# One fused decoder block on one core: a second home for transposed weights, later transposes, and the memory operands prepared elsewhere

## The chip, the cores and the metric

The kernel runs on one core of a Trainium2 chip. A core has TensorE (PE: matmuls, with a separate track PEld for loading the stationary operand), VectorE (DVE), ScalarE (ACT), GpSimd (POOL) and SyncE (SP, which here only issues DMAs). The metric is the device time of one execution in microseconds, as the median of several runs.

## The reference, cut to what matters

One layer over 512 positions of width 1024: self-attention with 16 heads of 64 (8 dilated, 8 block-sparse), a projection `w_out`, a cross-attention of 4 heads over 256 memory positions, and a gated MLP with a causal convolution, each with RMSNorm ahead and a residual add behind.

```python
u  = rmsnorm(h, g_mix);  qa, ka, va, qb, kb, vb = split(u @ w_in)
y  = concat([rmsnorm(dilated(qa, ka, va)), rmsnorm(moba(qb, kb, vb))])
h  = h + y @ w_out
m  = rmsnorm(mem, g_mem)                       # 256 x 1024
km, vm = split(m @ w_kv)                       # memory keys, memory values
h  = h + softmax((rmsnorm(h) @ w_q) km.T / 16) vm @ w_o
h  = h + (silu(conv3(rmsnorm(h) @ w_gate)) * (rmsnorm(h) @ w_up)) @ w_down
```

## The kernel before, in words

Everything is kept feature-major: a tile holds 128 features by 512 positions. Each fp32 operand is held as a rounded part (`hi`, fp32r, written by ACT) and a remainder (`lo`, written by DVE or POOL), and each product is three matmuls: hi by hi, hi by lo, lo by hi (`fgroup`, L263 to L268). Weights arrive in chunks of 128 x 1024 through three `stage` buffers; `Weights.tick` splits the next chunk beside the matmuls of the present one (ACT at L88, DVE or POOL at L97), and a finished split issues the DMA three chunks on. All of these DMAs, the bias strips (`load_strip`) and the copies of K go through SP's queue, in the order of the program.

The order on every engine is written out by hand (`manual_schedule`). What follows a matmul group, such as an evacuation, is put into a list, `Later`, and emitted a few steps further on; each group of matmuls is one `L.step()`.

**Self-attention** runs in 18 slots, one per head and two to finish. In slot s the head s has its scores made (S, three pieces: `s_steps`, L658, four score tiles), head s-1 its probabilities transposed (T, three groups of 4, 3 and 3 transposes: `t_steps`, L704), and head s-2 its output (O, four pieces: `o_steps`, L729). Between these stand steps of filler, as many as `PACE` prescribes: the projections `q1`, `k1` ... `k7`, two groups of V, then the memory keys `km0` to `km7` and the memory values `vm0` to `vm3`. The string `ORDER` says where in the slot each piece stands. Softmax of a score piece: DVE reduces (L683), ACT exponentiates (L688), DVE takes reciprocals (L693), and DVE (tiles 2 and 3) or POOL (tiles 0 and 1, the last piece) multiplies by them (L695). The first transposes need tiles 0 and 1. A transposed group is evacuated from PSUM into `pts`: ACT writes `pt0h`, `pt1h`, `pt2h` (L249), DVE `pt0l` and so on (L254). There is one set of `pts`; the O pieces of the head read it.

**Memory operands.** In the unit `k7` the two halves of the transposed memory come in as two chunks of the weight stream (`raw`), and `mem_prep(k)` scales and splits tile k into `X[k][:, 0, :]`, where the normalised stream has been until then, right after `k7` has read it (ACT L251, DVE L261). `km` units multiply these (moving width 256); `vm_unit(c)` takes two chunks of weights, makes 256 columns for two position tiles with 24 matmuls each, and evacuates each on its own. All fillers put their sums into two PSUM banks, tag `acc`; S, T, O and norms share a ring of six.

**After it** comes `w_out` (L819): per output tile a sum `pa` over the first four tiles of Y and `pb` over the last four. They are scaled by the two norms RA and RB, and added to the residual `h`: POOL L832 and DVE L840. RB is made inside this phase (`norm_stages`: two matmuls against ones, L301 and L302; the second waits for a DVE subtraction, L254). `h` is loaded once at the start and stays in memory for the whole kernel.

Of the kernel before, what the change touches and what calls it, by code (L numbers as in the profile page):

```python
# [31 lines left out]
ORDER = "OSOTOSTOST"  # L32
# [17 lines left out]
def bf(ap):  # L50
    return ap.bitcast(F32)
# [121 lines left out]
def block_kernel(tc, xT, x_tok, memT, mem_tok, w_in, w_out, w_q, w_km, w_vm, w_o, w_gu, w_dn, vecs, relT, onehot,  # L173
                 addend, out):
    nc = tc.nc
    with ExitStack() as ctx:
        perm = ctx.enter_context(tc.tile_pool(name="perm", bufs=1))
        wp = ctx.enter_context(tc.tile_pool(name="wp", bufs=1))
# [24 lines left out]
        chunks += [(memT[0], "raw"), (memT[1], "raw")]  # L203
# [17 lines left out]
        nc.sync.dma_start(h[0], xT[0])  # L221
        W.dma(0)
        nc.sync.dma_start(h[1], xT[1])
        W.dma(1)
        for k in (2, 3):
            nc.sync.dma_start(h[k], xT[k])
# [140 lines left out]
        def x_split(k):  # L367
            copy(Xh[k], h[k], col(C_MIX + k))
            scaled_lo(Xl[k], h[k], col(C_MIX + k), Xh[k])
# [40 lines left out]
        for k in range(KT):  # L410
            if k % 2 == 0:
                w = W.take()
            for j in XL.get(k, ()):
                nc.sync.dma_start(h[j], xT[j])
# [29 lines left out]

        Q, K, VM = {}, {}, {}
# [12 lines left out]
        def qk_unit(p, is_k):  # L458
            hook = p == 7 and is_k
            w = W.take()  # L460
            ps = bank("acc")
            for k in range(KT):
                if hook and k == 0:
                    mem_start()
                proj(w, k, ps, Xh[k], Xl[k])
                if hook:
                    L.chain(*mem_prep(k), d=1)
                yield
# [76 lines left out]
        def mem_start():  # L545
            W.lo_eng = tuple(engs[c] for c in LOM)
            VM["st"] = [W.raw(), W.raw()]

        def mem_prep(k):

            src = VM["st"][k // 4][:, (k % 4) * M:(k % 4) * M + M]
            hi, lo = X[k][:, 0, 0:M], X[k][:, 0, M:2 * M]
            return (lambda: copy(hi, src, col(C_MEM + k)),
                    lambda: scaled_lo(lo, src, col(C_MEM + k), hi))

        def km_unit(m):
            w = W.take()
# [16 lines left out]
        def vm_unit(c):  # L574
# [5 lines left out]
            w = [W.take(), W.take()]  # L580
            for t in range(2):
                ps = bank("acc")[:, :256]
                for k in range(KT):
                    wh, wl = w[k // 4]
                    ws = slice((k % 4) * 256, (k % 4) * 256 + 256)
# [685 lines left out]
```

## Time and profile before

| what | value |
|---|---|
| median of 3 runs | 796.68 us (796.01 to 797.83) |
| the profiled execution | 796.25 us |
| its span, first to last instruction | 794.5 us |
| PE busy, share of the span | 97% |
| DVE, ACT, POOL busy | 62%, 49%, 20% |
| mean granted TensorE clock | 0.997 |

The span is followed by lines for groups of instructions, waits and DMAs. A matmul's duration in the trace includes the time that it spends in the pipe behind others, so successive matmuls overlap, and their pace is read from start to start. A bracket behind a row is the time for which the engine stood idle before it and the instruction that ended the wait.

### The profile page before, as it was taken

Reading aid. Unit: us, or ns where it says so; the run is one execution under the profiler, and the core shown is the slowest. Engines: PE = TensorE matmul, PEld = TensorE weight load, DVE = VectorE, ACT = ScalarE, POOL = GpSimd, SP = SyncE. Lnnn points to the kernel's source line nnn. Section 1 sums busy time; section 2 is a strip of 40 time slices with the busy share of each in tenths; the row PEclk is TensorE's granted clock in tenths of the full one; section 3 lists DMA queues with packets and bytes.
Section 4 is the critical chain, followed back from the end, with each engine's and each line's share of the span. In section 5 each row is a group of like instructions: output and inputs, shape, how many; then the busy total and the mean of one; then the engine's idle time right before and its main releaser. Section 6 shows DMA issues by size and latency. Waiting matters only on the chain.

```text
span 794.5 us, 10594 instructions
## 1 busy us (share of the span) xinstructions
PE 772.7 (97%) x3916; PEld 653.9 (82%) x3916; DVE 491.7 (62%) x895; ACT 388.7 (49%) x763; POOL 162.6 (20%) x161
## 2 busy tenths in 40 slices
PE   9999999999999999999999999999999999999995
PEld 7878989877898887888888888888888888888884
DVE  4657676678886987756476765665665664333324
ACT  5856666776767543544355533334333343322322
POOL 1057465663646243000030000000000000000001
PEclk9999999999999999999999999999999999999998
DMA  9545243343534322211232323223223233333303
GB/s 344 198 133 138 78 145 93 109 112 123 161 134 131 108 80 85 75 53 54 80 106 92 104 97 106 99 87 104 91 98 106 88 92 100 99 93 100 99 21 106
DMA packets 27108, 85.86 MB, mean 108 GB/s; under 512 B 3072, under 2 KB 5248, under 8 KB 26672
## 3 DMA queue, kind: packets, MB, share of 16 engines
q1 hardware_dynamic: 25696, 83.90, 32.8%
q10 hardware_dynamic: 1232, 1.12, 0.4%
q8 instruction: 31, 0.51, 0.3%
q14 instruction: 21, 0.17, 0.1%
q0 software_dynamic: 128, 0.17, 0.1%
HBM read 78.84 MB, written 2.14 MB: 102 GB/s over the span
## 4 chain that ended last, share of the span: by engine, by line
PE 77%; DVE 11%; ACT 6%; issue 2%; POOL 2%; DMA 1%; DVEq 0%; POOLq 0%; ACTq 0%
PE acc L267 15%; PE acc L266 15%; PE acc L268 15%; PE s L267 6%; PE s L266 6%; PE s L268 6%; DVE lo L97 2%; ACT P L688 2%; PE o L739 1%; DVE tmp L257 1%; PE t L710 1%; DVE P L695 1%; DVE P L683 1%; ACT hi L88 1%; PE acc L531 1%
## 5 line engine op out<-in xcount | busy, mean ns | idle before, releaser
L88 ACT ACTIVATE hi<-stage 128x512 fp32r<-128x512 f32 (+1 forms) x264 | 151.9, 616 | 173.0 <-PE acc L267 126.6
L97 DVE TENSOR_TENSOR lo<-stage,hi 128x512 fp32r<-128x512 f32 (+1 forms) x211 | 154.8, 764 | 59.4 <-ACT hi L88 59.2
L266 PE MATMUL acc<-X,hi 128*128 128x512 f32 (+1 forms) x416 | 159.5, 384 | 1.1 <-DVE tmp L257 1.1
L268 PE MATMUL acc<-X,lo 128*128 128x512 f32 (+1 forms) x416 | 155.5, 374 | 0.0
L267 PE MATMUL acc<-X,hi 128*128 128x512 f32 (+1 forms) x368 | 137.3, 373 | 1.8 <-DVE X L261 1.5
L268 PEld LDWEIGHTS acc<-X,lo 128*128 128x128 f32 x416 | 78.2, 188 | 14.2
L266 PEld LDWEIGHTS acc<-X,hi 128*128 128x128 f32 x416 | 78.4, 188 | 13.8 <-ACT P L688 1.0
L267 PEld LDWEIGHTS acc<-X,hi 128*128 128x128 f32 x368 | 69.3, 188 | 13.1 <-DVE X L261 3.1
L97 POOL TENSOR_TENSOR lo<-stage,hi 128x512 fp32r<-128x512 f32 x53 | 71.6, 1368 | 27.3 <-ACT hi L88 25.7
L266 PE MATMUL s<-X,hi 128*128 128x512 f32 x192 | 75.1, 391 | 0.0
L268 PE MATMUL s<-X,lo 128*128 128x512 f32 x192 | 74.7, 389 | 0.0
L266 PE MATMUL acc<-G,hi 128*128 128x512 f32 (+1 forms) x198 | 72.9, 368 | 0.0
L268 PE MATMUL acc<-G,lo 128*128 128x512 f32 (+1 forms) x198 | 72.3, 365 | 0.0
L267 PE MATMUL acc<-G,hi 128*128 128x512 f32 (+1 forms) x198 | 72.3, 365 | 0.0
L267 PE MATMUL s<-X,hi 128*128 128x512 f32 x176 | 68.5, 389 | 0.0
L688 ACT ACTIVATE P<-P,st 128x512 f32<-128x512 f32 (+1 forms) x64 | 35.6, 557 | 39.9 <-DVE st L683 39.7
L1072 DVE SCALAR_TENSOR_TENSOR c<-a,vec,c 128x512 f32<-128x512 f32 x44 | 33.1, 752 | 25.2 <-ACT c L1067 24.4
L1062 POOL MEMSET a<- 128x2 f32 x22 | 2.1, 99 | 214.8 <-DVE c L1072 214.0
L266 PEld LDWEIGHTS acc<-G,hi 128*128 128x128 f32 x198 | 37.3, 188 | 6.2
L266 PEld LDWEIGHTS s<-X,hi 128*128 128x128 f32 x192 | 36.0, 187 | 7.7 <-issue 0.2
L268 PEld LDWEIGHTS acc<-G,lo 128*128 128x128 f32 x198 | 37.3, 188 | 6.1
L267 PEld LDWEIGHTS acc<-G,hi 128*128 128x128 f32 x198 | 37.3, 188 | 6.0
(249 smaller groups left out, 1498.8 us busy)
## 6 DMA issues: line engine op xcount, KB each, us to landing
stage<-in_w_gu_dram SPq DMA_DIRECT2D x44, 512.0 KB, 3.3
stage<-in_w_in_dram SPq DMA_DIRECT2D x23, 512.0 KB, 3.5
stage<-in_w_dn_dram SPq DMA_DIRECT2D x16, 512.0 KB, 3.5
strip<-scr SPq DMA_DIRECT2D x16, 256.0 KB, 3.6
stage<-in_w_km_dram SPq DMA_DIRECT2D x8, 512.0 KB, 3.3
stage<-in_w_vm_dram SPq DMA_DIRECT2D x8, 512.0 KB, 3.4
stage<-in_w_out_dram SPq DMA_DIRECT2D x8, 512.0 KB, 3.2
stage<-in_w_q_dram SPq DMA_DIRECT2D x8, 512.0 KB, 3.2
```

The costliest lines, as they stand in the source:

```text
L88: self.nc.scalar.activation(self.hi[i][:, a:b], self.stage[i][:, a:b], AF.Copy)
L97: self.lo_eng[part].tensor_sub(self.lo[i][:, a:b], self.stage[i][:, a:b], bf(self.hi[i][:, a:b]))
L257: nc.vector.tensor_mul(dst, a, b)
L266: nc.tensor.matmul(ps, wh[:, w0:w0 + P], xh, start=first, stop=False)
L267: nc.tensor.matmul(ps, wh[:, w0:w0 + P], xl, start=False, stop=False)
L268: nc.tensor.matmul(ps, wl[:, w0:w0 + P], xh, start=False, stop=last)
L531: nc.tensor.matmul(ps, Xh[k][:, ts], wh[:, ws], start=(k == 0), stop=False)
L683: nc.vector.tensor_tensor_reduce(v, src, sb[:, :n][:, ::-1], -0.125, 3e38, OP.add, OP.min, accum_out=st[:, i:i + 1])
L688: nc.scalar.activation(v, v, AF.Exp, scale=-1.0, bias=st[:, i:i + 1], accum_out=st[:, 4 + i:5 + i])
L695: engs[NME[i]].tensor_scalar(v, v, st[:, 8 + i:9 + i], None, op0=OP.mult)
L710: nc.tensor.transpose(ps[:, c * P:(c + 1) * P], pt[:, PO[i] + kb * P:PO[i] + (kb + 1) * P], ident)
L1072: nc.vector.scalar_tensor_tensor(v["c"], v["a"][:, 6 + o:6 + o + S], col(C_CW + o * FT + f), v["c"], op0=OP.mult, op1=OP.add)
```

## The change

`ORDER` puts the four O pieces of a slot ahead of the three T pieces. `pts` exists twice, and heads take turns. The memory no longer comes through the weight stream: four quarters of it are loaded into a small tile `mr` and split into a tile `XM` of its own, emitted 68, 90, 112 and 134 steps on in `Later`, between slots 3 and 7. `XM` takes the room of the input `x`, whose last reader is the split at the start; when the memory values are done, the room goes to `h`, which is loaded again from `xT`: eight DMAs on SP's queue, ahead of the loads that follow there. `vm_unit` has a moving width of 512: one chunk holds two tiles k of 512 columns, and the two position tiles have their sums open over four chunks, in the two `acc` banks for the first half and in two banks of the ring for the second. The norm RA has its stages 5 steps apart in place of 3. The scratch set aside for POOL's DMA descriptors is 2048 bytes.

```diff
-ORDER = "OSOTOSTOST"
+ORDER = "OOSOOTSTST"
...
-        chunks += [(memT[0], "raw"), (memT[1], "raw")]
...
-        hh_ = perm.tile([P, KT, S], F32, name="h")
-        h = [hh_[:, k, :] for k in range(KT)]
+        x_ = hp.tile([P, KT, S], F32, tag="H", name="x")
+        x = [x_[:, k, :] for k in range(KT)]
...
+        XM = hp.tile([P, KT, 2 * M], F32R, tag="H", name="xm")
+        def mem_prep(j):
+            v = {}
+            def p0():
+                v["t"] = tp.tile([P, 2 * M], F32, tag="mr", bufs=1, name=f"mr{j}")
+                nc.sync.dma_start(v["t"], memT[j // 2][:, (j % 2) * 2 * M:(j % 2 + 1) * 2 * M])
+            def p1(i):
+                hi, src = XM[:, 2 * j + i, 0:M], v["t"][:, i * M:(i + 1) * M]
+                copy(hi, src, col(C_MEM + 2 * j + i))
...
+            L.chain(p0, d=68 + 22 * j)
+            L.chain(lambda: p1(0), lambda: p2(0), lambda: p1(1), lambda: p2(1), d=80 + 22 * j, gap=2)
...
-                fgroup(ps, w, k, X[k][:, 0, 0:M], X[k][:, 0, M:2 * M], k == 0, k == KT - 1)
+                fgroup(ps, w, k, XM[:, k, 0:M], XM[:, k, M:2 * M], k == 0, k == KT - 1)
...
+            ps = {}
+            for j in range(4):
+                w = W.take()
+                for t in range(2):
+                    if j == 0:
+                        ps[t] = bank("acc" if c == 0 else "s")
+                    for i in range(2):
+                        k = 2 * j + i
+                        xh = XM[:, k, t * P:(t + 1) * P]
+                        xl = XM[:, k, M + t * P:M + (t + 1) * P]
+                        ws = slice(i * 512, i * 512 + 512)
+                        nc.tensor.matmul(ps[t], xh, w[0][:, ws], start=(k == 0), stop=False)
+                        nc.tensor.matmul(ps[t], xl, w[0][:, ws], start=False, stop=False)
+                        nc.tensor.matmul(ps[t], xh, w[1][:, ws], start=False, stop=(k == KT - 1))
...
+        pts = [[tuple(ap_.tile([P, n], F32R, name=f"pt{g}{z}{e}") for z in "hl")
+                for g, n in enumerate((512, 384, 512))] for e in range(2)]
...
-                ra_tok = L.chain(*norm_stages(SSQ[0], SSQ[0], S, 512), gap=3)
+                ra_tok = L.chain(*norm_stages(SSQ[0], SSQ[0], S, 512), gap=5)
...
+        hh_ = hp.tile([P, KT, S], F32, tag="H", name="h")
+        h = [hh_[:, k, :] for k in range(KT)]
+        for k in range(KT):
+            nc.sync.dma_start(h[k], xT[k])
...
-    nc = _bacc.Bacc("TRN2", target_bir_lowering=False, num_devices=1)
+    nc = _bacc.Bacc("TRN2", target_bir_lowering=False, num_devices=1, dynamic_dma_scratch_size=2048)
```

How this moves instructions is shown at three places. The first is PE in slot 2, up to the first transposes of head 1 (`t<-ident,P1`; `o<-pt..` are O pieces of head 0, `acc` rows are filler). Before:

```order
L739 MATMUL o_37_667<-pt1h_428,V0_137 128x384
L739 MATMUL o_37_667<-pt1l_429,V0_137 128x384
L266 MATMUL acc_35_644<-X5_111,hi9_553 128x512
L267 MATMUL acc_35_644<-X5_111,hi9_553 128x512
L268 MATMUL acc_35_644<-X5_111,lo9_587 128x512
L266 MATMUL acc_35_644<-X6_112,hi9_553 128x512
L267 MATMUL acc_35_644<-X6_112,hi9_553 128x512
L268 MATMUL acc_35_644<-X6_112,lo9_587 128x512
L710 MATMUL t_39_700<-ident_85,P1_573 128x128 x4
```

After the change, the same transposes:

```order
L750 MATMUL o_37_679<-pt2h0_434,V0_140 128x256
L750 MATMUL o_37_679<-pt2l0_435,V0_140 128x256
L552 MATMUL acc_40_731<-hi10_656,X0_109 128x256
L553 MATMUL acc_40_731<-hi10_656,X0_109 128x256
L554 MATMUL acc_40_731<-lo10_682,X0_109 128x256
L552 MATMUL acc_40_731<-hi10_656,X1_110 128x256
L553 MATMUL acc_40_731<-hi10_656,X1_110 128x256
L554 MATMUL acc_40_731<-lo10_682,X1_110 128x256
L721 MATMUL t_42_741<-ident_88,P1_590 128x128 x4
```

They stood behind the second O piece (`pt1`) and now stand behind the last (`pt2`).

The second place is DVE in slot 8, where head 7 is transposed and head 8 scored (`pt0l` and `pt1l` are the transposed remainders, `P` the score tiles). Before:

```order
L695 TENSOR_SCALAR P_1523<-P_1523,st_1524 128x512
L254 TENSOR_TENSOR pt0l<-t_1546,pt0h 128x512
L257 TENSOR_TENSOR tmp_1565<-acc_1485,rx_138 128x512
L683 ISA P_1523,st_1524<-s_1567,strip_1226 128x384
L683 ISA st_1524 128x1
L514 TENSOR_TENSOR Q_1557<-tmp_1565,Q_1557 64x512
L693 RECIPROCAL st_1524<-st_1524 128x1
L695 TENSOR_SCALAR P_1523<-P_1523,st_1524 128x384
L254 TENSOR_TENSOR pt1l<-t_1580,pt1h 128x384
```

After:

```order
L706 TENSOR_SCALAR P_1567<-P_1567,st_1568 128x512
L771 TENSOR_TENSOR y_1589<-o_1548,tmp_1590 64x512
L258 TENSOR_TENSOR tmp_1600<-acc_1522,rx_141 128x512
L535 TENSOR_TENSOR Q_1592<-tmp_1600,Q_1592 64x512
L694 ISA P_1567,st_1568<-s_1616,strip_1266 128x384
L694 ISA st_1568 128x1
L255 TENSOR_TENSOR pt0l_437<-t_1602,pt0h_436 128x512
L704 RECIPROCAL st_1568<-st_1568 128x1
L706 TENSOR_SCALAR P_1567<-P_1567,st_1568 128x384
```

The remainder `pt1l` stood behind the reciprocal and the multiplication of a score piece; now a remainder stands ahead of these two.

The third place is DVE at the end of self-attention (`vml` are memory values; the `ssy` rows and the two ahead of the first of them make the norm RA; the last row is the subtraction for RB's second matmul; the row before it is the first `pa` times RA). Before:

```order
L312 TENSOR_SCALAR tmp_2861<-tmp_2861 128x512
L257 TENSOR_TENSOR ssy_944<-tmp_2861,tmp_2860 128x512
L760 TENSOR_TENSOR y_2750<-o_2792,tmp_2884 64x512
L97 TENSOR_TENSOR lo_2899<-stage_2757,hi_2892 128x512
L261 SCALAR_TENSOR_TENSOR Y_124<-y_2750,vec,Y_124 128x512
L261 SCALAR_TENSOR_TENSOR vml<-acc_2864,small,vmh 128x256
L97 TENSOR_TENSOR lo_2935<-stage_2814,hi_2921 128x512 x2
L257 TENSOR_TENSOR tmp_2948<-acc_2919,ssy_944 128x512
L254 TENSOR_TENSOR tmp_2957<-ssy_1946,tmp_2946 128x512
```

After:

```order
L97 TENSOR_TENSOR lo_2803<-stage_2718,hi_2792 128x512
L262 SCALAR_TENSOR_TENSOR vml<-s_2690,small,vmh 128x512
L262 SCALAR_TENSOR_TENSOR vml<-s_2708,small,vmh 128x512
L312 SCALAR_TENSOR_TENSOR tmp_2814<-t_2783,tmp_2814 128x512
L313 TENSOR_SCALAR tmp_2814<-tmp_2814 128x512
L258 TENSOR_TENSOR ssy_909<-tmp_2814,tmp_2813 128x512
L97 TENSOR_TENSOR lo_2852<-stage_2752,hi_2840 128x512 x2
L258 TENSOR_TENSOR tmp_2865<-acc_2838,ssy_909 128x512
L255 TENSOR_TENSOR tmp_2874<-ssy_1946,tmp_2863 128x512
```

The three rows of RA and two wide evacuations now stand close ahead of RB's subtraction; before, RA was done ahead of the last evacuation of Y.

## Rows read from the trace of the kernel before

**Rows 1.** The page, section 1: busy time, share of the span, instructions.
```profile
PE 772.7 (97%) x3916; PEld 653.9 (82%) x3916; DVE 491.7 (62%) x895; ACT 388.7 (49%) x763; POOL 162.6 (20%) x161
```
**Rows 2.** Windows: length, busy (x count) PE, PEld, DVE, ACT, POOL, clock, DMA share, GB/s.
```profile
150.00:200.00 50.00, 46.87 (x256) 38.90 (x256) 37.94 (x91) 34.80 (x82) 25.79 (x23) 1.00 0.38 116
...
450.00:500.00 50.00, 50.00 (x222) 41.42 (x221) 30.88 (x47) 20.66 (x34) 0.49 (x5) 1.00 0.29 99
```
**Rows 3.** Waits: who waited for whom, us in total, times, longest.
```profile
PE t L710 <- POOL P L695: 4.0, 7, 0.8
...
PEld acc L267 <- DVE X L261: 3.1, 6, 1.0
...
PE acc L266 <- DVE tmp L257: 1.1, 2, 0.6
```
**Rows 4.** Timeline of PE, slot 1: start, duration, instruction, [idle before <- releaser].
```profile
56.73 0.39 PE L268 MATMUL acc<-X,lo 128*128 128x512 f32 x1
57.86 0.33 PE L710 MATMUL t<-ident,P 128*128 128x128 f32 x1 [0.75 <-POOL P L695]
58.77 0.44 PE L710 MATMUL t<-ident,P 128*128 128x128 f32 x2 [0.58 <-POOL P L695]
```
**Rows 5.** Timeline of PE, first memory keys.
```profile
190.41 0.28 PE L266 MATMUL acc<-X,hi 128*128 128x256 f32 x1
191.49 0.39 PE L267 MATMUL acc<-X,hi 128*128 128x256 f32 x1 [0.79 <-DVE X L261]
```
**Rows 6.** Lines by form, the memory's split: count, busy us, mean ns, idle before.
```profile
L261 DVE SCALAR_TENSOR_TENSOR X<-stage,vec,X 128x256 fp32r<-128x256 f32 x8 | 5.3, 688 | 0.5 <-ACT X L251 0.5
...
L251 ACT ACTIVATE X<-stage,vec 128x256 fp32r<-128x256 f32 x8 | 3.5, 497 | 0.0
```
**Rows 7.** Timeline of PE, the fourth memory-value sum begins.
```profile
240.89 0.34 PE L739 MATMUL o<-pt1l,V 128*128 128x384 f32 x1
242.79 0.38 PE L588 MATMUL acc<-hi,X 128*128 128x256 f32 x1 [1.57 <-DVE vml L261]
```
**Rows 8.** Timeline of PE, successive matmuls of 256 and of 512 columns.
```profile
228.90 0.28 PE L588 MATMUL acc<-hi,X 128*128 128x256 f32 x1
229.02 0.28 PE L589 MATMUL acc<-hi,X 128*128 128x256 f32 x1
...
500.07 0.39 PE L268 MATMUL acc<-X,lo 128*128 128x512 f32 x1
500.30 0.39 PE L266 MATMUL acc<-X,hi 128*128 128x512 f32 x1
```
**Rows 9.** Timeline of DVE: the last memory-key sum is read, its bank free.
```profile
231.59 0.41 DVE L257 TENSOR_TENSOR tmp<-acc,rm 128x256 f32<-128x256 f32 x1
```
**Rows 10.** Timeline of PE, `w_out`: its first matmul, and RB's second.
```profile
261.06 0.40 PE L266 MATMUL acc<-Y,hi 128*128 128x512 f32 x1
...
268.24 0.50 PE L302 MATMUL t<-tmp,ones 128*128 128x512 f32 x1 [0.64 <-DVE tmp L254]
```
**Rows 11.** Timeline of ACT: RA's reciprocal root.
```profile
255.71 1.28 ACT L306 ACT_TABLE_LOAD   x1
257.00 0.69 ACT L306 ACTIVATE tmp<-t,small 128x512 f32<-128x512 f32 x1
```
**Rows 12.** Timelines: head 8's second group transposed (PE), evacuated (DVE), read (PE).
```profile
158.59 0.38 PE L710 MATMUL t<-ident,P 128*128 128x128 f32 x2
...
161.61 0.54 DVE L254 TENSOR_TENSOR pt1l<-t,pt1h 128x384 fp32r<-128x384 f32 x1
...
164.35 0.33 PE L739 MATMUL o<-pt1h,V 128*128 128x384 f32 x1
```
**Rows 13.** DMA issues: count, KB each, median us to landing.
```profile
strip<-scr SPq DMA_DIRECT2D x16, 256.0 KB, 3.6
...
h<-in_xT_dram SPq DMA_DIRECT2D x8, 256.0 KB, 6.3
```
**Rows 14.** Timeline of POOL: the first residual add behind `w_out`.
```profile
267.66 1.66 POOL L832 TENSOR_TENSOR h<-h,tmp 128x512 f32<-128x512 f32 x1 [2.94 <-DVE tmp L257]
```

More of the change, by code (lines that the diff above doesn't have):

```diff
@@ L458, in qk_unit @@
         def qk_unit(p, is_k):
-            hook = p == 7 and is_k
             w = W.take()
@@ L542, in vb_unit @@
                 tok["v", g, t] = L.chain(*v_evac(V[g][t], ps, rcol[:, t:t + 1]))
[L545 to L554, printed above, removed]
         def km_unit(m):
+            if m == 0:
+                W.lo_eng = tuple(engs[c] for c in LOM)
             w = W.take()
@@ L579, in vm_unit @@
                 VM["lo"] = kp.tile([P, 2, D], F32R, tag="V", name="vml")
[L580 to L585, printed above, removed]
-                    xh = X[k][:, 0, t * P:(t + 1) * P]
-                    xl = X[k][:, 0, M + t * P:M + (t + 1) * P]
-                    nc.tensor.matmul(ps, xh, wh[:, ws], start=(k == 0), stop=False)
-                    nc.tensor.matmul(ps, xl, wh[:, ws], start=False, stop=False)
-                    nc.tensor.matmul(ps, xh, wl[:, ws], start=False, stop=(k == KT - 1))
-                    if t == 0:
-                        W.tick(k)
-                    if t == 1 and k in (5, 6, 7):
-                        for i in {5: (0, 1), 6: (3,), 7: (4,)}[k]:
-                            W.tick(i)
-                    if k % 2 == 1:
+            ps = {}
@@ new lines, in vm_unit @@
+            for j in range(4):
+                w = W.take()
[10 more added lines that the diff above has]
+                        nc.tensor.matmul(ps[t], xh, w[1][:, ws], start=False, stop=(k == KT - 1))
+                        W.tick((0, 1, 3, 4)[2 * t + i])
@@ L625, in block_kernel @@
         FILL += [(f"km{m}", km_unit(m)) for m in range(8)]
-        FILL += [(f"vm{c}", vm_unit(c)) for c in range(4)]
+        FILL += [(f"vm{c}", vm_unit(c)) for c in range(2)]
         fill_gen = fillers()
@@ L648, in block_kernel @@
                 pass
-        pts = [(ap_.tile([P, 512], F32R, name="pt0h"), ap_.tile([P, 512], F32R, name="pt0l")),
-               (ap_.tile([P, 384], F32R, name="pt1h"), ap_.tile([P, 384], F32R, name="pt1l")),
-               (ap_.tile([P, 512], F32R, name="pt2h"), ap_.tile([P, 512], F32R, name="pt2l"))]
-        for t in pts[2]:
-            nc.vector.memset(bf(t[:, 0:128]), 0.0)
+        pts = [[tuple(ap_.tile([P, n], F32R, name=f"pt{g}{z}{e}") for z in "hl")
+                for g, n in enumerate((512, 384, 512))] for e in range(2)]
+        for e in range(2):
+            for t in pts[e][2]:
+                nc.vector.memset(bf(t[:, 0:128]), 0.0)
         PT, stat = {}, {}
@@ L713, in t_steps @@
                 o = 128 if g == 2 else 0
-                hi, lo = (t[:, o:o + n] for t in pts[g])
+                hi, lo = (t[:, o:o + n] for t in pts[hh % 2][g])
                 def b0(hi=hi, ps=ps, n=n):
@@ L739, in o_steps @@
                     nc.tensor.matmul(ps[:, 512 - (b - a):512], V[g][kb][:, j * P:(j + 1) * P],
-                                     pts[pg][z][:, a:b], start=(kb == 0 and z == 0),
+                                     pts[e][pg][z][:, a:b], start=(kb == 0 and z == 0),
                                      stop=(kb == 3 and z == 1))
```

41 lines of the change are left out of this document (21 added, 20 removed).

## Prediction, made before the run

> **What bounds the kernel now.** The page's busy times come first: PE is busy for 97% of the span, no other engine for more than 62% [rows 1]. The reader should then see where PE is not dense, which the windows show. Where the MLP runs, 222 matmuls fill 50 us to the last tenth; between 150 and 200 us PE is idle for 3.1 of 50 us, while ACT and DVE are busy for 35 and 38 [rows 2]. The granted clock is 1.00 in both. So time is to be had in two ways only: fewer PE columns or instructions, and the holes in self-attention. The table of waits names those holes [rows 3], and the timelines say what one of them costs. A matmul of 512 columns starts 0.23 after the one before, and one of 256 columns 0.12 [rows 8]; with that, the first hole of slot 1 loses 57.86 - 56.73 - 0.23 = 0.90 us for a bracket of 0.75 [rows 4], and the largest at the memory keys 1.08 - 0.12 = 0.96 for 0.79 [rows 5]. A hole therefore costs its bracket and about 0.16.
>
> All sums are made against the profiled execution, 796.25 us with a span of 794.5; the median of the runs is 0.43 higher, and a change of the span is taken over to it.
>
> **Later transposes.** PE waits 7 times, 4.0 us in all, for POOL to multiply the last two score tiles [rows 3]; at 0.16 more each that is 5.1 us. Nothing is made faster on POOL, but the transposes come later. Counting the rows of the order between the last score piece of a head and its first transposes, at the durations of rows 8, the distance grows by 1.36 us in slot 1 and by 1.8 to 2.6 in every other. Slot 1 loses 0.90 and then, as the second tile comes late too, about 0.8 [rows 4], so some 0.4 stay there. The other waits are shorter than their shift. Gain: **4.7**.
>
> The price stands at the other end. A transposed group has to be evacuated by ACT and DVE before its O piece, and that distance shrinks: by the same count by 1.0 to 3.6 us over the 48 groups. In the trace, head 8's second group is transposed from 158.59, its remainder is done at 162.15, and O reads it at 164.35: 2.20 us to spare [rows 12], of which the change takes 2.05. Done for all 48 groups, which have 1.8 to 7.3 us to spare, this leaves one short (head 7's second, by 0.4) and 12 more with under 1 us. On DVE's side the new order helps: the remainder stood behind the reciprocal and the multiplication of a score piece and now stands ahead of them. The two sets of `pts` only take away a reason for the evacuation to wait. The cost lies between 0 and, with all groups 1 us later, 5 us (the worst group of each slot, added up); I take **0.4**, the value of the count, because the rows that moved ahead speak for less and not for more.
>
> **Memory operands.** Where the memory is split inside `k7` and `km0`, the weight loads for the memory keys wait 3.1 us for DVE [rows 3]. The split, 5.3 us on DVE and 3.5 on ACT [rows 6], moves to slots 3 to 7, 60 us long, onto engines that are busy for 76% and 70% even in the fuller window behind these slots [rows 2]; nothing on PE waits for it until the first memory keys. Gain **3.1**; what it delays in these slots is in the price above. The same crowd on DVE makes the third memory-key sum wait for its bank, a bracket of 0.6 [rows 3]: gain **0.75**. On SP's queue the four loads of `mr` stand among strips and weights; each waits for the DVE work on the one before, emitted four steps earlier, so that what stands behind it (a weight chunk, wanted two chunks later) may be some 2 us late. I put that at nothing.
>
> **Memory values of 512 columns.** 192 matmuls of 256 columns become 96 of 512: 96 x (2 x 0.119 - 0.227) = **1.1** us, with the spacing taken from longer runs of the rows of which rows 8 are two pairs. The Trainium skill ("TensorE: Matmul & The Clock Gate", Back-to-back issue gap) gives an isolated matmul at full clock N / 2.4 + 2.5 ns; worked out from that, an estimate, the gain would be 0.24 us, and the whole sum 0.9 less. The rows have 12 ns or so per matmul beyond the columns and not 2.5, so the trace does not agree.
>
> The evacuations in between go. One of them lost 242.79 - 240.89 - 0.18 = **1.7** us to a bank not yet read [rows 7]. In their place, the second sum of the first half begins only 2.05 us (counted rows) after the last memory-key sum ends, and takes that sum's bank. Before, that sum ended when L588 began, at 228.90 [rows 8], and its bank was read at 232.00 [rows 9], 3.1 us later. The wait is then about **1.0**; its bounds are 0 (DVE less crowded) and 1.6 (the slowest of the last five reads).
>
> **The end of self-attention.** RB's second matmul waits 0.64, which costs 0.80, and starts 7.2 us after `w_out`'s first matmul [rows 10]; without a wait it would be 6.4. In the new order RA's last stages and two wide evacuations stand close ahead. ACT: a table load of 1.28, then passes of about 0.7 [rows 11], two for the root and one for the second evacuation, 3.3 in all, from about 0.25 after `w_out` begins. DVE then: that evacuation 0.75, RA 1.8, a weight chunk 1.3, two more passes 1.35, together 5.2. RB's matmul comes 8.7 us after the beginning and loses 2.4: **1.6** more than before. The bounds are 0 and 2.4. Nothing follows on the banks: the third tile wants its own 10.9 us after the beginning.
>
> **h again.** Eight loads of 256 KB follow the last memory-value matmul. The first add wants `h[0]` 6.6 us into `w_out` before [rows 10, 14] and, by the sum above, some 8 after; a load of this size lands in 3.6 us (strips) or 6.3 (the same tiles in the crowd at the start) [rows 13]. Cost nothing. If that cover were gone, POOL and then DVE would stand, and PE only when the chunks behind on DVE run out, some 20 us into `w_out`. The smaller scratch touches only POOL's four DMAs, all issued ahead of the first slot: nothing.
>
> **The sum.** Gains 4.7 + 3.1 + 0.75 + 1.1 + 1.7 = 11.35; costs 0.4 + 1.0 + 1.6 = 3.0. Net 8.4 us: a profiled execution of 787.9, and a median of **788.3**.
>
> **The rivals.**
> 1. *The evacuated transposes become the bound.* O now follows T within 3.2 to 6.4 us. If the path from transposes to remainder becomes longer by 1 us throughout, by ACT and DVE being pushed closer together once PE no longer waits, O waits in most slots: 5.2 us, so a net gain of 3.6 and 793.1. At 1.5 us it is 10.5, and at 2 us 17.6. From about 1.6 us on the change is slower than before, about 799 (2 us longer would give 805). For it speak the 13 groups that have under 1 us left; against it the order of DVE, and PE being idle for 6% at most today.
> 2. *The transposes wait as before.* POOL also splits weights, and a product of tiles 0 and 1 behind one of these would come as late relative to the new place. Then 4.7 are lost: 792.9. Against it: POOL is busy for half of the time at most in these windows [rows 2] and the distance is a row count.
> 3. *The reload is late.* The Trainium skill ("DMA: Bandwidth & Descriptors", Queues, rings and completion order) says that completions are not first-in first-out for an issuing engine, so `h[0]` may land with the last of the eight. No row here shows it; the loads at the start had 6.3 at the median, in a crowd. Late by 5 us it would delay the residual chain of `w_out` and cost PE perhaps 2 where the next phase waits for the last tile: 790.3.
>
> **How the numbers follow.** The forecast (net 6 to 11.35) has 0.70, rival 1 below its turning point 0.12, and beyond it 0.06, rival 2 0.07, rival 3 0.05. The range reaches from no costs at all, 796.68 - 11.35 = 785.3, with 0.5 below it for unnamed small holes, to rival 1 at 1 us, 793.1. A difference of 0.2% (1.6 us) is about what a measurement can tell from no change. Rival 1 passes through that band: half of its 0.18 is still faster, 0.05 within it, 0.04 slower; with a little for what is not seen, faster 0.88, same 0.06, slower 0.06.
>
> **What would show it.** In the profile after: PE's wait of transposes for POOL under 0.8 us in all, none for DVE's split of the memory, one of about 1 us at the first memory values, one of about 2.2 at RB, and PE x3820 in place of x3916. Waits of `o` for `pt` of more than 3 us in all would make the first rival right. A wait of POOL's or DVE's residual add for a DMA would be the third.

## The result, and the profile after

| what | before | after |
|---|---|---|
| median of 4 runs | 796.47 us (796.01 to 797.83) | 790.45 us (789.83 to 791.02) |
| the profiled execution, its span | 796.25, 794.5 | 790.84, 789.0 |

The ratio is 0.9922, with an interval of 0.991 to 0.9934: 6.0 us faster, where 8.4 were forecast, inside the forecast range. The kernel before was timed again beside each group of experiments, and its executions lie in two groups, 795.9 to 796.8 us and 797.3 us or more, so that its median was 797.73 beside four of the experiments (the change without its new order, one home, the remainders earlier, all weight remainders on DVE) and 796.31 or 796.37 beside the others; each ratio below is against the median measured beside it. The line numbers of after are shifted: transposes L721 (L710), outputs L750 (L739), POOL's and DVE's product of score tiles L706 (L695), the transposed remainders L255 (L254), scaled remainders L262 (L261), RB's matmuls L302 and L303 (L301 and L302).

The page's busy times of after answer to [rows 1]. There are 96 matmuls fewer, and DVE, ACT and POOL are as busy as before to within 2 us:

```profile
PE 770.6 (98%) x3820; PEld 650.4 (82%) x3820; DVE 491.6 (62%) x892; ACT 387.8 (49%) x759; POOL 164.5 (21%) x162
```

The table of PE's waits in after answers to [rows 3] (who waited for whom: us in total, times, longest):

```profile
PE o L750 <- DVE pt0l L255: 1.8, 1, 1.8
PE t L303 <- DVE tmp L255: 1.6, 1, 1.6
PE acc L552 <- DVE V L262: 1.2, 1, 1.2
...
PE o L750 <- DVE pt1l L255: 0.6, 2, 0.4
...
PE o L750 <- DVE pt2l L255: 0.4, 1, 0.4
```

The transposes' waits for POOL and the memory keys' waits for DVE are gone from it. New are outputs that wait for transposed remainders, and a value sum of the attention itself (L552) that waits for an evacuation.

To compare whole executions I took PE's timeline and summed, at each place, the time from one matmul's start to the next beyond the dense spacing of its columns (0.227 us for 512, 0.179 for 384, 0.119 for 256, 0.088 for 128, from long runs of these traces). The first line is the number of matmuls times that spacing, so it repeats the count of the forecast and doesn't test it. The other lines depend by some tenths of a us on which small gaps are counted. Differences are taken before rounding:

| us of PE's time | before | after | difference | forecast |
|---|---|---|---|---|
| dense work | 754.5 | 753.5 | -1.1 | -1.1 |
| transposes wait for POOL | 5.6 | 0 | -5.6 | -4.7 |
| memory keys wait for DVE | 3.9 | 0 | -3.9 | -3.85 |
| memory values, waits for a bank | 1.7 | 0 | -1.7 | -1.7 + 1.0 |
| outputs wait for transposed weights | 0 | 3.4 | +3.4 | +0.4 |
| RB's second matmul | 0.8 | 1.8 | +1.0 | +1.6 |
| attention's value sums | 1.1 | 2.5 | +1.4 | 0 |
| matmuls at half the clock | 0 | 1.6 | +1.6 | 0 |
| all else (start, end, small gaps) | 16.7 | 16.1 | -0.6 | 0 |
| sum | 784.3 | 778.9 | -5.4 | -8.4 |

The gains came to 12.3 us, where 11.35 were forecast. The prices came to 7.4 where 3.0 stood: outputs, RB, value sums, clock.

The largest hole of after belongs to head 12. The first fence is PE's timeline (start, duration, instruction, [idle before it <- releaser]), the second DVE's and the third POOL's, of the same time:

```profile
201.38 0.60 PE L721 MATMUL t<-ident,P 128*128 128x128 f32 x4
...
206.88 0.39 PE L750 MATMUL o<-pt0h,V 128*128 128x512 f32 x1
209.05 0.50 PE L750 MATMUL o<-pt0l,V 128*128 128x512 f32 x1 [1.77 <-DVE pt0l L255]
...
209.50 0.28 PE L268 MATMUL acc<-xm,hi 128*128 128x256 f32 x1
209.62 0.28 PE L269 MATMUL acc<-xm,lo 128*128 128x256 f32 x1
...
210.60 0.41 PE L269 MATMUL acc<-xm,lo 128*128 128x256 f32 x1
210.81 0.41 PE L267 MATMUL acc<-xm,hi 128*128 128x256 f32 x1
```

```profile
202.54 0.69 DVE L771 TENSOR_TENSOR y<-o,tmp 64x512 f32<-64x512 f32 x1
203.27 0.42 DVE L258 TENSOR_TENSOR tmp<-acc,rm 128x256 f32<-128x256 f32 x1
204.03 0.75 DVE L262 SCALAR_TENSOR_TENSOR Y<-y,vec,Y 128x512 fp32r<-128x512 f32 x1 [0.34 <-ACT Y L252]
204.70 1.79 DVE L97 TENSOR_TENSOR lo<-stage,hi 128x512 fp32r<-128x512 f32 x1
206.41 1.50 DVE L255 TENSOR_TENSOR X<-tmp,X 128x256 fp32r<-128x256 f32 x1
207.84 0.55 DVE L694 CUSTOM_DVE_ANT_0 P<-s,strip 128x384 f32<-128x384 f32 x1
...
208.31 0.68 DVE L255 TENSOR_TENSOR pt0l<-t,pt0h 128x512 fp32r<-128x512 f32 x1
```

```profile
204.60 1.34 POOL L282 TENSOR_TENSOR ssy<-ssy,tmp 128x512 f32<-128x512 f32 x1 [2.97 <-ACT tmp L277]
205.90 1.73 POOL L97 TENSOR_TENSOR lo<-stage,hi 128x512 fp32r<-128x512 f32 x1
```

The transposes end at 201.98 and their remainder at 208.99, 7.0 us later. DVE stands still for 0.34 us in that time; it works through the evacuation of the head before (`y`, `Y`), a weight chunk, a memory key and a score piece, and only then reaches the remainder. Two of these rows last 1.79 and 1.50 us where the same forms take 0.68 and 0.42 elsewhere. Only the second of them is new, as DVE's timeline of before shows ahead of the same remainder:

```profile
206.62 1.78 DVE L97 TENSOR_TENSOR lo<-stage,hi 128x512 fp32r<-128x512 f32 x1
208.32 0.41 DVE L254 TENSOR_TENSOR X<-tmp,X 128x256 fp32r<-128x256 f32 x1
208.66 0.68 DVE L254 TENSOR_TENSOR pt0l<-t,pt0h 128x512 fp32r<-128x512 f32 x1
```

Behind the hole, 256 columns take 0.21 us from start to start instead of 0.12. The windows of after show the clock there (the granted clock is the third number from the end); 0.50 is 1.2 GHz:

```profile
208.00:210.00 2.00, 0.95 (x7) 0.91 (x8) 1.79 (x8) 1.57 (x5) 0.00 (x0) 0.99 0.65 242
210.00:212.00 2.00, 2.00 (x11) 2.00 (x10) 1.68 (x6) 2.00 (x8) 0.28 (x1) 0.50 0.05 20
212.00:214.00 2.00, 2.00 (x11) 1.90 (x11) 1.36 (x4) 1.56 (x4) 2.00 (x3) 0.65 0.00 0
214.00:216.00 2.00, 2.00 (x19) 2.00 (x18) 1.94 (x4) 0.82 (x2) 2.00 (x2) 1.00 0.00 0
```

### The profile page after: what moved, and what is told of

Same layout as the page of the kernel before. It is cut to its first block, busy times and chain, and to the rows that moved or that the text cites. A ratio compares the mean times of both kernels' runs of the same rounds, so it can differ in the third digit from the quotient of the medians.

```text
span 789.0 us, 10400 instructions
## 1 busy us (share of the span) xinstructions
PE 770.6 (98%) x3820; PEld 650.4 (82%) x3820; DVE 491.6 (62%) x892; ACT 387.8 (49%) x759; POOL 164.5 (21%) x162
## 4 chain that ended last, share of the span: by engine, by line
PE 82%; DVE 9%; ACT 4%; DMA 2%; issue 2%; POOL 1%; DVEq 0%; SPq 0%; ACTq 0%; POOLq 0%
PE acc L267 17%; PE acc L269 17%; PE acc L268 17%; PE s L267 6%; PE s L268 6%; PE s L269 6%; DVE lo L97 2%; PE o L750 2%; DMA mr<-in_memT_dram 2%; PE t L721 1%; DVE tmp L258 1%; PE s L688 1%; PE s L689 1%; POOL h L847 1%; ACT X L252 1%
## 5 line engine op out<-in xcount | busy, mean ns | idle before, releaser
L97 DVE TENSOR_TENSOR lo<-stage,hi 128x512 fp32r<-128x512 f32 x210 | 153.3, 761 | 59.1 <-ACT hi L88 58.8
L267 PE MATMUL acc<-X,hi 128*128 128x512 f32 x352 | 140.5, 399 | 0.5 <-DVE tmp L258 0.5
L269 PE MATMUL acc<-X,lo 128*128 128x512 f32 x352 | 137.5, 391 | 0.0
L268 PE MATMUL acc<-X,hi 128*128 128x512 f32 x304 | 118.6, 390 | 0.0
L269 PEld LDWEIGHTS acc<-X,lo 128*128 128x128 f32 x352 | 66.1, 188 | 14.3
L97 POOL TENSOR_TENSOR lo<-stage,hi 128x512 fp32r<-128x512 f32 x54 | 73.9, 1384 | 14.9 <-ACT hi L88 13.8
L267 PEld LDWEIGHTS acc<-X,hi 128*128 128x128 f32 x352 | 66.1, 188 | 12.3 <-DVE tmp L258 0.9
L268 PEld LDWEIGHTS acc<-X,hi 128*128 128x128 f32 x304 | 57.2, 188 | 9.8 <-issue 0.2
L699 ACT ACTIVATE P<-P,st 128x512 f32<-128x512 f32 (+1 forms) x64 | 35.7, 558 | 30.2 <-DVE st L694 29.9
```

Of the source, the lines that this page charges most:

```text
L97: self.lo_eng[part].tensor_sub(self.lo[i][:, a:b], self.stage[i][:, a:b], bf(self.hi[i][:, a:b]))
L267: nc.tensor.matmul(ps, wh[:, w0:w0 + P], xh, start=first, stop=False)
L268: nc.tensor.matmul(ps, wh[:, w0:w0 + P], xl, start=False, stop=False)
L269: nc.tensor.matmul(ps, wl[:, w0:w0 + P], xh, start=False, stop=last)
L699: nc.scalar.activation(v, v, AF.Exp, scale=-1.0, bias=st[:, i:i + 1], accum_out=st[:, 4 + i:5 + i])
```

## Experiments: do the parts add up?

**The change without its new order.** All parts but one.

```diff
-ORDER = "OOSOOTSTST"
+ORDER = "OSOTOSTOST"
```

> The changed kernel with the old order of steps in a slot (transposes in places 4, 7 and 10 again instead of 6, 8 and 10); all else as changed. Theory A (the later transposes gained their 5.5 us, and gave back 3.4 us in attention outputs that wait for the transposed weights, and some 2 us more in the profiled run by the clock that fell behind the longest of these waits): the transposes wait for GpSimd's normalisation again, 4 to 6 us in all, the outputs' waits for the transposed weights are under 0.6 us, and the clock stays at 0.99 or more everywhere behind 50 us; the time is within 1.5 us of the changed kernel's 790.5 (789.5 to 792). Theory B (the prediction's sum: the later transposes are worth 4.7 against 0.4): 794 to 795.

Measured: 798.03 us, 1.0012 of before (1.0003 to 1.0022). The waits of this kernel:

```profile
PE t L721 <- POOL P L706: 5.8, 8, 1.7
PE t L303 <- DVE tmp L255: 2.9, 1, 2.9
```

The transposes wait as the first theory said, and no output waits. But neither theory gave the time: RB's matmul lost 3.2 us, and behind this hole and one of 1.8 us at 119 us the clock fell (its mean between 270 and 276 us is 0.55), 4.4 us more in the profiled execution. Without the new order, all the rest of the change gains nothing.

**The new order alone,** on the kernel before.

```diff
-ORDER = "OSOTOSTOST"
+ORDER = "OOSOOTSTST"
```

> The kernel before with the new order of steps in a slot alone (transposes in places 6, 8 and 10). The run with the old order showed the rest of the change alone at 798.0, no gain over before. Theory A (the parts add up: the order is worth the 7.3 us by which 798.0 and the changed kernel's 790.5 differ): 789 to 790.5, that is at least as fast as the whole change. Theory B (the parts need each other: with the memory's splits still at the last query-key unit, waits for VectorE take their place, and the outputs wait for the transposed weights): no wait of the transposes for GpSimd, three waits of the km sums for VectorE's remainders as before (3 us), the mid wait of the memory values (1.7 us) as before, outputs' waits for transposed weights of 2 to 4 us: 793 to 796.

Measured: 798.49 us, 1.0024 of before (1.0015 to 1.0032). Both theories fall; it is slower than either. The waits for POOL are gone, and these stand in their place (waits, then the largest in PE's timeline):

```profile
PE acc L266 <- DVE vml L261: 3.9, 1, 3.9
PE o L739 <- DVE pt0l L254: 2.1, 1, 2.1
PE o L739 <- DVE pt1l L254: 1.7, 2, 1.3
```

```profile
258.44 0.28 PE L590 MATMUL acc<-lo,X 128*128 128x256 f32 x1
262.63 0.50 PE L266 MATMUL acc<-Y,hi 128*128 128x512 f32 x1 [3.91 <-DVE vml L261]
```

`w_out`'s first sum waits for the bank of the last memory values. DVE's timeline tells why:

```profile
258.34 0.75 DVE L261 SCALAR_TENSOR_TENSOR Y<-y,vec,Y 128x512 fp32r<-128x512 f32 x1 [2.49 <-ACT Y L251]
259.11 0.69 DVE L311 SCALAR_TENSOR_TENSOR tmp<-t,tmp 128x512 f32<-128x512 f32 x1
259.83 0.68 DVE L312 TENSOR_SCALAR tmp<-tmp 128x512 f32<-128x512 f32 x1
260.54 1.64 DVE L257 TENSOR_TENSOR ssy<-tmp,tmp 128x512 f32<-128x512 f32 x1
262.10 0.47 DVE L261 SCALAR_TENSOR_TENSOR vml<-acc,small,vmh 128x256 fp32r<-128x256 f32 x1
```

The three stages of the norm RA (L311, L312, L257) stand ahead of the remainder that frees the bank. On ACT the table load for RA's root (1.28 us from 255.05) held up `Y`, whose copy begins at 257.60, in the same way.

**The new order with RA's stages farther apart.** If that reading is right, the one number that the change moved from 3 to 5 takes the wait away.

```diff
-ORDER = "OSOTOSTOST"
+ORDER = "OOSOOTSTST"
...
-                ra_tok = L.chain(*norm_stages(SSQ[0], SSQ[0], S, 512), gap=3)
+                ra_tok = L.chain(*norm_stages(SSQ[0], SSQ[0], S, 512), gap=5)
```

> The kernel before with the new order of steps and with RA's stages 5 steps apart instead of 3; nothing else. The run with the order alone (798.5) waited 3.9 us at the first w_out sum for the last remainder of the memory values, with RA's ScalarE and VectorE stages (255.0 to 262.1 us) ahead of it in the queues. Theory A (RA's place makes that wait): it falls to under 0.5 us, the wait of the second RB matmul is 1.2 to 1.8 us: 794.5 to 796.5. Theory B (the last values' evacuation is late by itself under the new order): 3 us or more stay, 797.5 or above.

Measured: 793.66 us, 0.9966 of before (0.9952 to 0.998). The wait at `w_out` is gone, RB's is 1.2, and the clock stays at 1.00 in every window of 50 us. First theory; the time is 0.8 below its band.

**The change with narrow memory values and RA's stages 3 apart,** both as before. The second cover is the second pair of banks: with it, `w_out`'s first sum finds a bank that was read long ago.

```diff
...
-                ra_tok = L.chain(*norm_stages(SSQ[0], SSQ[0], S, 512), gap=5)
+                ra_tok = L.chain(*norm_stages(SSQ[0], SSQ[0], S, 512), gap=3)
...
-        "w_vm": _rows(kv[:, D:], 2, 512),
+        "w_vm": _rows(kv[:, D:], 4, 256),
```

The part left out ahead of these lines gives `vm_unit` its old loop, reading `XM`.

> The changed kernel with the memory values 256 columns wide through one pair of banks and RA's stages 3 apart, both as before; the order, the memory operands in slots 3 to 7 and the rest as changed. Each of the two alone cost 1.1 us and nothing. Theory A (either of the two keeps the first w_out sum from waiting for the memory values' last evacuation, and without both the wait of 3.9 us comes back): 3 us or more of wait at the first w_out sum, the second RB matmul without a wait over 0.5: 793 to 796. Theory B (the two costs add up): 791.3 to 792.

Measured: 796.13 us, 0.9993 of before (0.9984 to 1.0002), and the wait is back:

```profile
PE acc L267 <- DVE vml L262: 3.9, 1, 3.9
```

First theory (its band ended 0.13 below). Each of the two reverted alone is measured in the section on the other prices: 791.56 and 790.68. Together they cost 5.7 and not 1.3, since each covers the same hole.

The same table for the kernels of this section, in us of PE's time:

| place | before | order alone | order, RA 5 apart | all but the order | all (after) |
|---|---|---|---|---|---|
| transposes for POOL | 5.6 | 0 | 0 | 7.6 | 0 |
| outputs for transposed weights | 0 | 4.2 | 4.2 | 0 | 3.4 |
| memory keys | 3.9 | 2.7 | 2.7 | 0 | 0 |
| banks of memory values | 1.7 | 4.9 | 1.0 | 1.0 | 0 |
| RB | 0.8 | 0 | 1.4 | 3.2 | 1.8 |
| half the clock | 0 | 3.3 | 0 | 4.4 | 1.6 |
| median | 796.5 | 798.5 | 793.7 | 798.0 | 790.5 |

If the two parts added up (0.12% and 0.24% slower), both together would have been some 3 us slower than before; they are 6.0 faster. No run takes the memory operands alone out of the change: they are in the step from the order with RA 5 apart to all (793.7 to 790.5), together with the wide memory values.

## Experiments: the outputs' waits

**One home for the transposed weights.**

```diff
-                hi, lo = (t[:, o:o + n] for t in pts[hh % 2][g])
+                hi, lo = (t[:, o:o + n] for t in pts[0][g])
...
-                                     pts[e][pg][z][:, a:b], start=(kb == 0 and z == 0),
+                                     pts[0][pg][z][:, a:b], start=(kb == 0 and z == 0),
```

> The changed kernel with one home for the transposed weights of all heads instead of two; all else as changed. Theory A (in the new order all four output steps of a slot stand ahead of its first transpose, so that a copy into the home finds it read out already): no copy waits for TensorE's outputs, and the time is within 0.5 us of the changed kernel's 790.5. Theory B (the second home is what lets the copies run early): ScalarE's copies of the transposed weights wait for the outputs, the outputs' waits for the remainders grow by 1 us or more, 792 or above.

Measured: 790.71 us, 0.9912 of before (0.9893 to 0.9932), the same as after, and no copy that waits for an output. The first theory: the second home does nothing. Its profiled execution, 793.56, is the slowest of its four: the clock falls there behind head 12's hole and again behind RB's, which is 2.5 us, and that costs 1.5 and 1.6 us.

**The remainders two steps earlier in DVE's queue.**

```diff
-GT = (1, 3)
+GT = (1, 1)
```

> The changed kernel with the remainders of the transposed weights issued one step behind their ScalarE copy instead of three steps behind it (two steps earlier in VectorE's queue). Theory A (the outputs wait because the remainder stands too late in VectorE's queue): the outputs' waits for the transposed weights fall from 3.4 us in all to 1.5 or less, and the clock doesn't fall at 210 us: 786 to 789. Theory B (VectorE is the bound there: its rows are stretched and its queue late by itself, so that a place in it changes little, and a remainder at the front of it only stands waiting for its copy): the waits stay within 1 us of 3.4, 790 to 792.

Measured: 804.19 us, 1.009 of before (1.0075 to 1.0106), 13.7 slower than after, with the clock at 1.00. Both theories were far off. The outputs lose some 11 us instead of 3.4, and the value sums 5.9 instead of 2.5. DVE's waits between 50 and 260 us, first of after, then of this kernel:

```profile
DVE st L704 <- ACT P L699: 19.6, 38, 1.4
```

```profile
DVE st L704 <- ACT P L699: 31.3, 41, 1.4
...
DVE pt0l L255 <- ACT pt0h L250: 3.7, 10, 0.6
...
DVE pt2l L255 <- ACT pt2h L250: 2.5, 11, 0.4
```

As the second theory said, a remainder at the front of the queue stands there until ACT has made its copy (6.2 us in all, where after has 1.2). What stands behind it is late for ACT in turn, and DVE's waits for ACT's exponentials (L699) grow by 11.7 us: two engines that hand work to each other in order lose on both sides. The second theory had the mechanism and not its size.

**All weight remainders on DVE,** from the second memory-key chunk on.

```diff
-LOM = "vg"
+LOM = "vv"
```

> The changed kernel with the remainder of every weight chunk behind the first km chunk computed by VectorE alone instead of half by VectorE and half by GpSimd. Theory A (the hole at 207 us comes from VectorE rows that take 1.5 to 1.8 us while GpSimd runs beside them, where they take 0.4 to 0.7 alone): the rows of that line stay at 0.7 to 0.8 us on VectorE, the output of head 12 waits under 0.6 us, the clock doesn't fall there: 787 to 789.5. Theory B (VectorE has too much work there by itself): with 0.7 us more in every chunk the outputs' waits grow: 791 to 794.

Measured: 789.82 us, 0.9904 of before (0.9888 to 0.9919). In the trace the hole of head 12 shrinks from 1.94 to 0.75 us and the clock stays at 1.00 there; in the medians the gain of 0.6 is too small to tell. It is the first theory, 0.3 above its band, though DVE has more to do. One row does not follow it, since POOL's sum of squares (204.16 to 205.50) still runs beside it (DVE's timeline; the next weight chunk, without POOL, takes 0.68):

```profile
204.25 1.79 DVE L97 TENSOR_TENSOR lo<-stage,hi 128x512 fp32r<-128x512 f32 x1
205.97 0.41 DVE L255 TENSOR_TENSOR X<-tmp,X 128x256 fp32r<-128x256 f32 x1
```

## Experiments: the other prices

**RA's stages 3 apart in the changed kernel.**

```diff
-                ra_tok = L.chain(*norm_stages(SSQ[0], SSQ[0], S, 512), gap=5)
+                ra_tok = L.chain(*norm_stages(SSQ[0], SSQ[0], S, 512), gap=3)
```

> The changed kernel with the stages of the first output norm (RA) 3 steps apart again, as before, instead of 5. Theory A (the second norm's wait, RB, comes from RA's late stages, which push the VectorE work behind them): the wait of the second RB matmul falls from 1.6 to 0.6 to 0.9 us, 789.3 to 789.9. Theory B (the wait comes from the rest of VectorE's queue there, with the memory values' remainders at 512 columns): 1.4 us or more stay, 790.2 to 791.

Measured: 790.68 us, 0.9925 of before (0.9912 to 0.9938); RB waits 1.75. The second theory. With 3 steps and with 5 the same rows stand ahead of RB's subtraction on DVE: the two wide remainders, RA's three stages, three weight chunks and the first product with RA. The number only decides which of them come first. In after DVE stands ahead of the second of the wide remainders until ACT has made its copy, and from there works without a pause up to the subtraction:

```profile
257.81 0.75 DVE L262 SCALAR_TENSOR_TENSOR vml<-s,small,vmh 128x512 fp32r<-128x512 f32 x1 [2.15 <-ACT vmh L252]
```

**The memory operands one piece earlier.**

```diff
-            L.chain(p0, d=68 + 22 * j)
-            L.chain(lambda: p1(0), lambda: p2(0), lambda: p1(1), lambda: p2(1), d=80 + 22 * j, gap=2)
+            L.chain(p0, d=46 + 22 * j)
+            L.chain(lambda: p1(0), lambda: p2(0), lambda: p1(1), lambda: p2(1), d=58 + 22 * j, gap=2)
```

> The changed kernel with the loads and the splits of the memory operands one piece (22 steps) earlier, so that none lies at 117 to 122 us. Theory A (the 1.4 us hole at 128 us, where a value sum waits for the evacuation of the one two sums before it, comes from the two memory remainders of 1.5 and 0.5 us in VectorE's queue at 120 and 122 us): the hole falls to 0.5 or less, no new one over 0.5 us: 789 to 789.8. Theory B (the hole comes from the remainders of the transposed weights that stand ahead of the value's remainder): the hole stays at 1.0 or more, 790 to 791.

Measured: 788.64 us, 0.9899 of before (0.9886 to 0.9912). The same value sum in PE's timeline, in after and in this kernel:

```profile
129.28 0.35 PE L552 MATMUL acc<-hi,X 128*128 128x256 f32 x1 [1.15 <-DVE V L262]
```

```profile
128.57 0.36 PE L552 MATMUL acc<-hi,X 128*128 128x256 f32 x1 [0.38 <-DVE V L262]
```

The first theory: the memory's remainders at 120 and 122 us made most of that hole. By the spacing it loses 0.54 instead of 1.41; the 1.8 by which the medians differ is more than that, and no run shows how much of the rest is the clock. The hole of head 12 stays (1.94), and here the clock stays at 1.00 behind it, as it does in the profiled executions with RA 3 apart and with narrow values: a hole of that size does not bring the clock down each time.

**Memory values of 256 columns,** all else as changed; the first mark stands for the old loop of `vm_unit`, reading `XM`.

```diff
...
-        "w_vm": _rows(kv[:, D:], 2, 512),
+        "w_vm": _rows(kv[:, D:], 4, 256),
```

> The changed kernel with the memory values in four units of 256 columns through one pair of banks, as before; all else as changed. Theory A (the prediction's two terms, 1.1 for the width and 1.7 for the wait for an evacuation in the middle): PE work up by 1.1 us, a wait of 1.5 to 2 us for a remainder of the memory values, 793 to 793.6. Theory B (that wait came from the old order, and only the width is left): 791.3 to 791.9.

Measured: 791.56 us, 0.9941 of before (0.9929 to 0.9954): 1.1 more than after. The time is the second theory's, but not for its reason: a wait in the middle of the values is left, 0.63 us, not 1.57; RB waits 1.2 instead of 1.6. So the 1.1 is not the width alone.

**Three holes closed.** Earlier memory, all weight remainders on DVE, and RB's matmuls two groups later:

```diff
-LOM = "vg"
+LOM = "vv"
...
-            L.chain(p0, d=68 + 22 * j)
+            L.chain(p0, d=46 + 22 * j)
...
-        rb_tok = L.chain(*norm_stages(RB, RB, S, 512), d=RBD, gap=2)
+        rb_tok = L.chain(*norm_stages(RB, RB, S, 512), d=RBD, gap=3)
...
-            last = L.chain(f1, f2, *resid(m, ss1, Xh[m], HL[m], C_CROSS), d=6 if m == 0 else 1)
+            last = L.chain(f1, f2, *resid(m, ss1, Xh[m], HL[m], C_CROSS), d=10 if m == 0 else 1)
```

> The changed kernel with the memory operands one piece earlier, all weight remainders from the second km chunk on VectorE, and the second output norm (RB) with stages 3 apart instead of 2, so that its matmuls stand two more groups (1.4 us) later behind w_out's first sum; the first residual add waits 10 steps for it instead of 6. Theory A (the three holes are separate: 0.9 at 128 us, 1.2 at 207 us, 1.4 at 260 us, of which the first two gave 1.8 and 0.6): 785.8 to 787. Theory B (the third only moves the wait to the sums that need RB): 787.3 to 788.5.

Measured: **785.92 us**, 0.9864 of before (0.9851 to 0.9878), 4.5 below after and the fastest of all. RB's wait in PE's timeline answers to [rows 10]:

```profile
259.77 0.50 PE L303 MATMUL t<-tmp,ones 128*128 128x512 f32 x1 [0.27 <-DVE tmp L255]
```

The time is the first theory's, by which the three holes are separate. In the trace they fall from 1.41, 1.94 and 1.79 to 0.51, 0.74 and 0.44. No run closes the third alone.

**POOL's sums of squares on DVE** as well.

```diff
-                add(nc.gpsimd, SSQ[p // 4], v["s"])
+                add(nc.vector, SSQ[p // 4], v["s"])
```

> The kernel with those three changes, and the six sums of squares in the attention's outputs added by VectorE (0.7 us each) instead of GpSimd (1.3 us each). Theory A (the VectorE row of 1.8 us at 204 us is slow because GpSimd adds beside it): that row takes 0.7 us, the output of head 12 waits for no remainder there, and 0.3 to 0.8 us are gained on the kernel with the three changes. Theory B (the row is slow by itself): it stays at 1.5 us or more, and VectorE's added work costs 0 to 1 us.

Measured: 786.37 us, 0.9871 of before (0.9857 to 0.9884). DVE's timeline at the same place, with nothing running on POOL:

```profile
203.26 0.68 DVE L282 TENSOR_TENSOR ssy<-ssy,tmp 128x512 f32<-128x512 f32 x1
203.86 0.68 DVE L97 TENSOR_TENSOR lo<-stage,hi 128x512 fp32r<-128x512 f32 x1
```

The row takes 0.68 us, and head 12's output loses 0.25 us instead of 0.74, as the first theory has it. Its gain doesn't come: other outputs now wait (0.4 us at 113, 0.6 at 161), and the medians are 0.45 apart the wrong way, within their intervals. So the cause of the slow row is shown, and removing it in this way is worth nothing.

## Why the prediction was right, and where its sum was not

The sign and the range held, and the terms that removed something were well sized. The sum was 2.4 too high by the medians, 2.9 by the trace, and its form, a list of independent terms, was wrong. In the trace three prices were missed or too small: outputs by 3.0, value sums by 1.4, the clock by 1.6. Errors the other way gave 3.1 of these 6.0 back: the transposes (0.9 more gained), the second bank (1.0 less), RB (0.6 less) and all else (0.6). That the time lies so well inside the range is in part luck.

- **Later transposes,** 4.7 forecast: 5.6 us gone in the trace, with slot 1 too. But this is no gain that stands by itself: the order alone made the kernel 2 us slower, and with RA's stages 5 apart it is 2.7 faster.
- **Outputs for transposed weights,** 0.4 forecast, 3.4 measured: this is the mis-sized step. The distance from transposes to outputs was counted rightly, for head 12 from 8.9 to 5.5 us. The time from transposes to remainder was taken from before, and that was wrong: for head 12 it went from 3.6 (transposed until 205.76, remainder done at 209.34 in the trace of before) to 7.0. The step "the rows that moved ahead speak for less and not for more" looked at the score piece that moved behind the remainder, and not at the evacuation of the previous head (`y`, `Y`), which the new order puts between transposes and remainder; the rows of slot 8 under "The change" already show `y` ahead of `pt0l`. Another 1.1 us of the path is POOL's doing: a memory key's subtraction ran beside POOL's weight chunk and took 1.50 instead of 0.41, and with that chunk on DVE the hole is 0.75. So the first rival came true, below its turning point, for four groups and not for all: three of them by 0.3 to 0.6 us, one by 1.9. The sign set for it, waits of more than 3 us, is not quite met by the table of waits (2.8) and is met by the losses (3.4). The turning point itself was put too high: by the rival's own costs, 5.2 us at 1 us and 10.5 at 1.5, the change loses from about 1.3 us on and not from 1.6.
- **Memory out of `k7`,** 3.85 with the third sum's bank: 3.9 in the trace. "What it delays in these slots is in the price above" was too cheap: the value sums lost 1.4 us more, and moving the splits 22 steps earlier took 0.9 off the largest of these holes and 1.8 off the median.
- **512 columns,** 1.1: in the trace the memory values' own matmuls take 23.5 us before and 22.6 after, summed from each start to the next, 0.9 less. The estimate of 0.24 worked out from the Trainium skill ("TensorE: Matmul & The Clock Gate", Back-to-back issue gap) does not hold here.
- **The mid wait,** 1.7: gone, though not by the width alone, since with 256 columns 0.8 is lost there in the new order.
- **The second bank,** 1.0: no wait at all; its lower bound was right. The count was made on a trace of the old order, and with the old order the wait is there: 0.93 us at 232 us in the run of all but the order.
- **RB,** 1.6 more: 1.0 more; its matmul came 8.1 us after `w_out`'s first (262.80 against 254.66), where 8.7 were worked out. The mechanism is the forecast's: DVE waits for ACT's copy of the last memory values and then works without a pause up to RB's subtraction. But that RA is later is not what delays it, since 3 steps give the same. What the 5 steps are worth was missed: under the new order they keep RA from standing ahead of the last memory values (4.8 us of medians between order alone and order with 5). The change brings two covers for that hole, so neither shows when taken away alone.
- **The clock** stood in no term. In the profiled execution of before, whose longest hole in the attention is 1.7 us, the clock is at 1.00 from 4.5 to 789.5 us; after lost 1.6 us. Each profile is one execution, and where the clock falls in the other executions of a kernel is not shown.
- **The second and the third rival** are out: no transpose waits for POOL, and POOL's residual add waits for no DMA. Its waits in after are all for DVE, with the `h` loads landing in 4.9 us at the median:

```profile
POOL h L847 <- DVE tmp L258: 17.2, 8, 6.2
```

What stays open: why the clock falls behind a hole of some 2 us in one execution and not in another, and what makes the three smaller of the outputs' waits.

## What to carry to other kernels

When an instruction group is moved on the engine that sets the time, list again on the engines that serve it what now stands between its result and its reader; a latency measured in the old order is not a number of the new one. Try the parts of a change together before dropping one that loses alone, and look for one hole with two covers where undoing either costs nothing. A remainder moved to the front of an in-order queue before its input is ready makes everything behind it late.

## What the runs showed of the hardware

A DVE instruction with two operands in SBUF takes far longer when a POOL instruction with two such operands is already running: weight chunks of 0.68 us took 1.79, and a subtraction of 0.42 took 1.50. In after, the DVE row of 1.79 begins 0.1 us after POOL's add and ends at 206.49, 0.55 after that add has ended (205.94): little less than its normal duration. So it goes in 23 of the 24 rows of after (weight chunks and these subtractions) that begin beside such a POOL row: each ends 0.55 (weight chunk) or 0.28 us (subtraction) after POOL's row. The one exception, at 219.02, took 0.68, and there POOL's row took 1.95, where such rows of POOL take 1.38 in the mean. The 25 that began ahead of a row of POOL took no longer than usual, nor did the 14 transposed remainders, one operand of which is in PSUM (0.55 to 0.69). The Trainium skill ("SBUF — State Buffer", Who interferes with whom) says that a VectorE instruction with two inputs in SBUF contends with a GpSimd instruction that reads SBUF, since its second input comes through a read interface that both share. The rows agree for POOL's instructions with two operands; beside POOL's product of a score tile, with one, the subtraction took 0.42 three times and a weight chunk 0.83 once. With the POOL add gone the row is 0.68.

A hole of some 2 us or more on a PE that is dense on either side can be followed by matmuls at 1.2 GHz. In these traces the clock falls nine times between 50 and 700 us, each time in or just behind a hole of 1.8 us or more, and stays there for 3 to 7 us, which costs 1.5 to 2.8 us. For the hole of head 12 (1.9 to 2.3 us where nothing was done against it) this came in the profiled executions of after, of one home, of the order alone and of narrow values with RA 3 apart, and not in those of five others; RB's holes of 1.8 to 1.9 us were not followed by it in five executions. The four holes of 2.5 to 4.1 us (one home, order alone, all but the order, narrow values with RA 3 apart) all were.
